# The merge of two mLSTM directions: reciprocal denominators spread by TensorE and applied by VectorE in place of GpSimd

## The chip, the cores and the metric

The kernel runs on one core of a Trainium2 chip. The metric is the device time of one execution in microseconds (us); lower is better. The engines of the core are named as in the profile: PE is TensorE's matmuls and PEld its weight loads, DVE is VectorE, ACT is ScalarE, POOL is GpSimd, SP is SyncE, which here issues the loads of the weights.

## The reference

One layer of a hybrid encoder over 272 positions (16 learned meta tokens and 256 of the sequence), model width 2048, float32. Its output is the 256 sequence positions after a last norm.

```
u = RMSNorm(h); proj = u @ W_in            # q/k, v, o, gates of A; q, k, v of B; two branch gates
branch A: bidirectional mLSTM, 4 heads x 256
branch B: differential attention, 8 heads
merged = sigmoid(g_A) * (A @ W_A) + sigmoid(g_B) * (B @ W_B);  h += merged @ W_out
h += ConvGLU(RMSNorm(h))
```

What matters here is one head of branch A. The reference steps through chunks of 64 positions; over the whole sequence this comes to a matrix of weights for each direction, whose entry for query t and key s is (q_t . k_s) / 16 times a decay. With `den` the sum of a query's weights over the keys,

```
h_fwd[t] = sum_s S_fwd[t, s] v[s] / max(|den_fwd[t]|, exp(-m_fwd[t]))      # s <= t
h_bwd[t] = the same with its own decay, sum, m and keys s >= t
hs = h_fwd + h_bwd;   hn = (hs - mean(hs)) * rsqrt(var(hs) + eps) * norm_g
```

So each direction's weights are divided by a denominator that belongs to the query and the direction, and then both can be added and multiplied by the values in one product.

## The kernel before

**Tiling.** Everything is kept transposed, feature on the partitions and position along the row. Projections are products of a weight block with the layer's input: the weights come as a stream of 512 KB pieces in a fixed order, loaded by SP's queue, split into a high and a low float32r part (`split`: ScalarE casts the high part, L157, VectorE subtracts for the low part, L115), and each 128x128 block takes three matmuls (high x high, high x low, low x high; `product`, L172). One piece of a projection of 256 columns is 24 matmuls. `prepare` splits three pieces ahead of their use, and a raw buffer becomes free for the next load when its low part is done.

**Stages.** `weave` runs two generators step by step, a part of the mLSTM or of the attention in front and a projection behind: each `yield` of the front lets one piece of the projection be traced. The stages in order: queries and keys with the decay terms, values with the heads' weights and their sums (`heads1`), then **`heads2`, the stage of the change, beside the attention's query projection** (`roped(dq, ...)`, 16 pieces in four blocks), then the attention's keys and values, its heads beside the branch gates, the output gate, the merge of the branches, `w_out`, and the FFN. Instructions are issued on each engine in an order that a planner settles when the kernel is built, from the order of the trace and a simulation with its own costs; each engine serves its own list strictly in that order, and semaphores make it wait for others.

**One head's weights.** `FB` is a row of 1034 columns on 128 key partitions that holds six blocks [key, query], three for each direction, one for each key tile (16 meta tokens, two tiles of 128 positions): `PARTS_W` lists column, key tile, first query and width of each: F0 258 wide, F1 256, F2 128, B2 258, B1 130, B0 2 (F0 and B0 on 16 partitions). Queries start at position 14, so there are `NT` = 258. `sums` adds each head's weights over the keys by TensorE into the PSUM tile `den`, head h on partition 32 h, both directions side by side.

**`heads2`.** `rec` = 1 / max(|den|, exp(-m)) is made once for all heads (ScalarE's Abs L665, VectorE's maximum L666 and reciprocal L667). Then for each head:

- `merged`: GpSimd broadcasts partition 32 h of `rec` to all partitions (`rc`, L627) and multiplies each of the six blocks by its stretch of `rc` (six `TENSOR_TENSOR`s on `FB`, which the profile puts at L161, the line of the helper `mul`). VectorE adds the blocks that belong to the same key tile (L164, L634), and the 774 columns that result are split into `hl` (L157 and L115).
- `outputs`: 18 matmuls of values by `hl` into `num`, a tile `two` of PSUM (a pool of two buffers of two banks each). ScalarE squares it (L647) and casts the square's high part (L648), GpSimd subtracts for the low part (L649).
- `normed`: 4 matmuls sum the squares over the partitions (`one`), `rsqrt` follows (ScalarE L151, VectorE L313 to L316), and VectorE multiplies `num` by gain and factor (L660).

The order in the trace is: `merged(0)`, two pieces, and for each head `outputs(h)`, `merged(h + 1)`, two pieces, `normed(h)`, two pieces. `hl` has one buffer.

**Beside it** a block of the query projection ends with `roped`: ScalarE copies out of the accumulator (L692), VectorE shuffles (L696), GpSimd multiplies by the sine table (`u<-u` at L161), VectorE multiplies by the cosine table, adds and splits. So GpSimd's work of the stage is broadcasts and products on `FB`, rope products, and the squares' low parts.

Of the kernel before, what the change touches and what calls it, by code (L numbers as in the profile page):

```python
# [10 lines left out]
F32 = mybir.dt.float32  # L11
# [12 lines left out]
LAM_INIT = 0.2  # L24
# Queries, gates and everything behind them are needed from position 15 on (the last meta token
# reaches position 16 through the FFN's convolution); an even width starts at 14.
T0 = 14
NT = L - T0
FF = 5632
NEG = -1e30  # L30
# Token tiles on partitions: the meta tokens, then the sequence's two halves.
ST = [(0, 16), (16, 128), (144, 128)]
# Columns of the constants' array.
C_ID, C_SEL, C_RC, C_RS, C_E = 0, 128, 640, 912, 1184
C_N = 1186
# Columns of w_in.
Q0, K0, V0, O0, G0 = 0, 1024, 2048, 3072, 4096
DQ0, DK0, DV0, GM0, GD0 = 4112, 5136, 6160, 7184, 9232
# The mLSTM's weights of one head, a [key, query] block per direction (F, B) and key tile, in one row:
# F0 | two columns, F1 | B2 make up the merged weights of the three key tiles; F2, B0, B1 go into them.  # L40
F0c, F1c, B2c, F2c, B0c, B1c, WN = 0, 260, 516, 774, 902, 904, 1034
# [23 lines left out]
def hybrid_layer(ctx, tc, x, meta, norm1_g, w_in, conv_w, gate_bias, mnorm_g, lq1, lk1, lq2, lk2,  # L65
# [26 lines left out]
    def pair(n):  # L92
        """Two 128-row tiles of an operand in two float32r parts."""
        return unit([2, n], F32R), unit([2, n], F32R)
# [22 lines left out]
    @contextmanager  # L117
    def in_order():
        """What is traced inside is issued in its order, engine by engine."""
        traced = nc.cur_bb.bb.instructions  # L120
        start, last = len(traced), {}
        yield
        for i in traced[start:]:
            if i.engine in last:
                behind(i, last[i.engine])
            last[i.engine] = i
# [8 lines left out]
    def activation(out, in_, func, **kw):  # L135
        """Functions of different tables keep the order in which they are traced: few loads of tables."""
        k = KIND[func]
        if k != table[0]:
            before, since[:] = since[:], []
            table[0] = k  # L140
            if k == 0:
                first = S.preload_act_table_set("natural_log_exp_and_others").ins
                for i in before:
                    behind(first, i)
                before = [first]
                since.append(first)
            a = S.activation(out, in_, func, **kw)
            for j in before:
                behind(a.ins, j)
        else:  # L150
            a = S.activation(out, in_, func, **kw)  # L151
            behind(a.ins, since[0])
        since.append(a.ins)
        return a
# [11 lines left out]
    def product(o, terms, first=True, last=True):  # L166
        """o += sum of a.T b, for operands in two parts (an exact one has a single part)."""
        ops = []
        for a, b in terms:
            ops += [(a[0], b[0])] + ([(a[0], b[1])] if len(b) > 1 else []) + ([(a[1], b[0])] if len(a) > 1 else [])  # L170
        for i, (p, q) in enumerate(ops):
            PE.matmul(o, p, q, start=first and i == 0, stop=last and i == len(ops) - 1)  # L172

# [1 line left out]
    blocks = [(w_in, 16, Q0 + 256 * b, 256, 4) for b in range(1, 4)]  # L175
# [57 lines left out]
    def gemm(src, kt, c0, ncols, xs, t0, nt, evac):  # L233
        """Columns c0.. of src, transposed: [column, token]; a generator that stops between pieces."""
        nk = 1024 // ncols
# [23 lines left out]

# [1 line left out]
    table[0] = 0  # L261
# [40 lines left out]
    ones = onesr.bitcast(F32)  # L302
    # a window of 128 columns of it has ones in one column
    selr = const.tile([P, 224], F32R, name="selr")
# [3 lines left out]
    def rsqrt(r, ss, n, work, bias=eps):  # L308
        """1 / sqrt(ss / n + bias), the tables' value and one step of Newton's."""
        a, t = work  # L310
        activation(r, ss, AF.Ln, bias=bias, scale=1.0 / n)
        activation(r, r, AF.Exp, scale=-0.5)
        V.tensor_scalar(out=a, in0=ss, scalar1=1.0 / n, scalar2=bias, op0=ALU.mult, op1=ALU.add)  # L313
        V.scalar_tensor_tensor(out=t, in0=r, scalar=-0.5, in1=r, op0=ALU.mult, op1=ALU.mult)
        mul(t, t, a)
        V.scalar_tensor_tensor(out=r, in0=t, scalar=1.5, in1=r, op0=ALU.add, op1=ALU.mult)  # L316

# [1 line left out]
    n1gT = const.tile([P, 16], F32, name="n1gT")  # L319
# [32 lines left out]
    with in_order():  # L352
# [5 lines left out]
        for k in range(16):  # L358
# [11 lines left out]
            if k == 10:  # L370
                # the gates' 16 columns: both parts side by side
                split(wg[:, :, 0:16], wg[:, :, 16:32], graw)
# [31 lines left out]

# [1 line left out]
    qs, ks = [], []  # L406
# [21 lines left out]

# [1 line left out]
    gsb = r1(L)  # L430
# [6 lines left out]
    def decay_terms():  # L437
        # rows 32 h of [:, direction, :]: head h; the other rows are idle
        pli, plf = two(), two()
# [5 lines left out]
        S.copy(li, pli[:, :, :L])  # L445
        # log_sigmoid(f) = min(f, 0) - log1p(exp(-|f|)), with what 1 + e rounds off given back
        S.activation(e, lf, AF.Abs)
# [13 lines left out]
        yield  # L461
        # m_t = max(lf_t + m_{t-1}, li_t) from 0; the second direction runs backwards
        V.tensor_tensor_scan(out=m[:, 0, :], data0=lf[:, 0, :], data1=li[:, 0, :], initial=0.0, op0=ALU.add, op1=ALU.max)
        V.tensor_tensor_scan(out=m[:, 1, ::-1], data0=lf[:, 1, ::-1], data1=li[:, 1, ::-1], initial=0.0,
                             op0=ALU.add, op1=ALU.max)
        yield
        # rows to broadcast: per key tile, (sum of lf from the tile's edge to t) - m_t
        V.memset(rows[:, 258:260], 0.0)
# [37 lines left out]

# [1 line left out]
    def values(c0, centred):  # L508
# [3 lines left out]
        def put(b):  # L512
# [5 lines left out]
            def turn():  # L518
# [6 lines left out]
                if centred:  # L525
                    # heads' values less their mean over the head: what follows is linear in them
                    mu = sm(3)
# [25 lines left out]

# [1 line left out]
    W, den = [], two()  # L555
# [22 lines left out]
    def scores(h):  # L578
# [3 lines left out]
        for s, (s0, n) in enumerate(ST):  # L582
            # 128 keys for the meta tokens too, whose first 16 rows are used
            product(sc[s], [([t[:, c, s0:s0 + P] for t in ks[h]], [t[:, c, :] for t in qs[h]]) for c in range(2)])
# [35 lines left out]

# [1 line left out]
    hn = []  # L622

    def merged(h, rec):
        FB = W[h]
        rc = t2([2, NT])
        G.partition_broadcast(rc, rec[32 * h:32 * h + 1, :, :])  # L627
        for d, parts in enumerate(PARTS_W):
            for at, s, q, n in parts:
                r = ST[s][1]  # L630
                mul(FB[0:r, at:at + n], FB[0:r, at:at + n], rc[0:r, d, q:q + n], G)
        add(FB[0:16, F0c:F0c + 2], FB[0:16, F0c:F0c + 2], FB[0:16, B0c:B0c + 2])
# [30 lines left out]
    def heads2():  # L663
# [3 lines left out]
        V.reciprocal(rec, rec)  # L667
        hl = merged(0, rec)
        yield
        yield  # L670
        for h in range(4):
            o = outputs(h, hl)
            if h < 3:
                hl = merged(h + 1, rec)
            yield
            yield
            normed(h, *o)
            yield
            yield

# [1 line left out]
    shuffle = [i + 8 if i < 8 else i - 8 if i < 16 else i for i in range(32)]  # L682
# [27 lines left out]

    # lam / max(|lam|, 1) and 1 / max(|lam|, 1): the norm behind takes a scale of its input, eps scaled with it
    lv = t2([4, 64])
# [16 lines left out]
    def softmax(ps, nrow, nmap):  # L729
        """exp(scale (s - max)) and the rows' 1 / sum, for maps [:, m, :] of ps."""  # L730
        p = t2([nmap, L])
# [11 lines left out]
    def position15():  # L743
        """Position 15's queries of all heads and maps at once, on 16 rows; its weights twice, for 14's too."""
        qb = [r1(P, F32R) for _ in range(2)]
# [87 lines left out]

# [1 line left out]
    def gates(dst, c0):  # L835
# [25 lines left out]

# [1 line left out]
    ms = []  # L863
# [20 lines left out]

# [1 line left out]
    hs = []  # L886
# [55 lines left out]

# [1 line left out]
    fc = t2([3, P])  # L944
# [118 lines left out]
```

## Time and profile before

| what | value |
|---|---|
| median of 3 runs | 1638.91 us |
| lowest and highest run | 1638.21, 1639.12 us |
| span of the profiled execution, first to last instruction | 1636.8 us |
| TensorE busy | 1578.3 us, 96% |
| VectorE busy | 1028.0 us, 63% |
| ScalarE busy | 763.5 us, 47% |
| GpSimd busy | 75.7 us, 5% |
| mean granted TensorE clock | 0.981 of full |
| read from HBM | 270.42 MB, 166 GB/s over the span |

The span is the only time that the profile gives for its own execution; the median of the runs is 2.1 us above it, for what lies around the span. Busy time is an average over stages with different limits, and a busy TensorE is not one at its peak, so the stage of the change has to be looked at by itself. In the views, "<- name" behind a wait is what ended it; "issue" means that nothing the profile shows did. PEclk is the clock that TensorE was granted, as a share of full speed (in tenths on the page).

### The profile page before, as it was taken

What the parts mean: (1) busy time and instruction counts of PE and PEld (TensorE: products, weight loads), DVE (VectorE), ACT (ScalarE), POOL (GpSimd) and SP (SyncE); (2) the same over time, 40 slices, a digit from 0 to 9 for tenths busy, and PEclk for the clock granted to TensorE, in tenths of its full rate; (3) what the DMA queues carried; (4) which work ended last, traced back from release to release, by engine and by line L of the source; (5) the groups of instructions that cost most, each with busy time, mean ns of one, the idle gap of its engine ahead of it and who ended that gap; (6) DMA issues with size and microseconds to landing.
All of it is one profiled execution on the core that took longest, in us unless ns stands there. A gap on an engine that the chain in (4) does not pass through costs nothing.

```text
span 1636.8 us, 28921 instructions
## 1 busy us (share of the span) xinstructions
PE 1578.3 (96%) x11862; PEld 1510.2 (92%) x11862; DVE 1028.0 (63%) x1595; ACT 763.5 (47%) x1135; POOL 75.7 (5%) x99
## 2 busy tenths in 40 slices
PE   8999975699999999999999999999999999999998
PEld 7999974699999999999999999999888999999887
DVE  6876644485788655566556766667544566766544
ACT  5656422343455543445555444444433454445433
POOL 0220012110000000000110000000000000000000
PEclk9999986899999999999999999999999999999999
DMA  7464421365445566555555566655555656565562
GB/s 236 135 201 140 132 75 52 92 181 169 129 118 169 181 182 181 181 180 181 189 181 175 180 188 182 185 182 187 184 177 196 189 181 186 179 189 181 178 198 101
DMA packets 254505, 274.39 MB, mean 168 GB/s; under 512 B 11396, under 2 KB 231925, under 8 KB 254357
## 3 DMA queue, kind: packets, MB, share of 16 engines
q1 hardware_dynamic: 248962, 268.99, 53.6%
q10 hardware_dynamic: 5411, 3.56, 0.8%
q8 instruction: 93, 1.52, 0.4%
q14 instruction: 39, 0.32, 0.1%
HBM read 270.42 MB, written 2.10 MB: 166 GB/s over the span
## 4 chain that ended last, share of the span: by engine, by line
PE 82%; issue 14%; POOL 2%; DVE 0%; DMA 0%; ACT 0%; POOLq 0%; SPq 0%; DVEq 0%
PE acc L172 78%; PE two L172 1%; POOL FB L161 1%; PE two L778 1%; POOL FB L564 0%; PE two L900 0%; PE one L790 0%; POOL u L161 0%; DMA xc<-in_x_dram 0%; PE two L333 0%; POOL t L627 0%; POOL t L649 0%; POOL FB L561 0%; PE two L911 0%; PE one L172 0%
## 5 line engine op out<-in xcount | busy, mean ns | idle before, releaser
L172 PE MATMUL acc<-u,hi 128*128 128x258 f32 (+1 forms) x6656 | 1226.8, 286 | 1.3 <-ACT u L692 1.3
L172 PEld LDWEIGHTS acc<-u,hi 128*128 128x128 f32 x6656 | 1037.6, 191 | 5.5 <-ACT u L692 1.9
L172 PE MATMUL acc<-u,lo 128*128 128x258 f32 (+1 forms) x3328 | 938.3, 285 | 1.9 <-DVE lo L115 1.9
L115 DVE TENSOR_TENSOR lo<-raw,hi 128x1024 fp32r<-128x1024 f32 x499 | 615.3, 1235 | 439.9 <-ACT hi L157 437.9
L157 ACT CAST hi<-raw 128x1024 fp32r<-128x1024 f32 x499 | 523.0, 1049 | 649.6 <-PE acc L172 502.2
L172 PEld LDWEIGHTS acc<-u,lo 128*128 128x128 f32 x3328 | 628.1, 190 | 3.7 <-DVE lo L115 3.0
L172 PE MATMUL acc<-hi,u 128*128 128x512 f32 (+1 forms) x704 | 210.6, 382 | 0.0
L172 PEld LDWEIGHTS acc<-hi,u 128*128 128x128 f32 x704 | 129.8, 188 | 27.7
L172 PE MATMUL acc<-lo,u 128*128 128x512 f32 (+1 forms) x352 | 134.5, 382 | 0.0
L172 PEld LDWEIGHTS acc<-lo,u 128*128 128x128 f32 x352 | 66.2, 188 | 14.6
L172 PE MATMUL two<-hl,v 16*128 16x258 f32 x24 | 8.2, 429 | 41.0 <-ACT hl L157 41.0
L161 DVE TENSOR_TENSOR r<-acc,r 128x258 f32<-128x258 f32 x88 | 37.3, 423 | 13.6 <-PE acc L172 13.6
L172 PEld LDWEIGHTS two<-hl,v 16*128 16x128 f32 x24 | 5.0, 253 | 43.4 <-ACT hl L157 41.8
L157 ACT CAST u<-r 128x256 fp32r<-128x256 f32 (+2 forms) x93 | 34.7, 405 | 12.6 <-DVE r L161 7.0
L115 DVE TENSOR_TENSOR u<-r,u 128x256 fp32r<-128x256 f32 (+2 forms) x93 | 37.7, 436 | 3.9 <-ACT u L157 3.3
L959 ACT ACTIVATE r<-r,fcT 128x256 f32<-128x256 f32 x88 | 39.8, 500 | 0.0
L960 DVE SCALAR_TENSOR_TENSOR r<-r,fcT,r 128x256 f32<-128x256 f32 x88 | 38.5, 479 | 0.0
L961 DVE SCALAR_TENSOR_TENSOR r<-r,fcT,r 128x255 f32<-128x255 f32 x88 | 38.5, 479 | 0.0
L157 ACT CAST hl<-FB 128x1034 fp32r<-128x1034 f32 (+1 forms) x8 | 7.6, 945 | 54.4 <-DVE FB L164 48.0
L151 ACT ACTIVATE r<-r 128x256 f32<-128x256 f32 (+2 forms) x77 | 29.6, 413 | 5.7 <-DVE r L419 5.3
L164 DVE TENSOR_TENSOR FB<-FB 128x128 f32<-128x128 f32 (+1 forms) x12 | 4.8, 412 | 41.6 <-POOL FB L161 41.6
L164 POOL TENSOR_TENSOR ssum<-ssum,r 128x258 f32<-128x258 f32 x15 | 13.4, 896 | 318.5 <-ACT r L927 318.0
(232 smaller groups left out, 767.7 us busy)
## 6 DMA issues: line engine op xcount, KB each, us to landing
raw<-in_w_in_dram SPq DMA_DIRECT2D x176, 512.0 KB, 3.7
raw<-in_w_up_dram SPq DMA_DIRECT2D x176, 512.0 KB, 3.6
raw<-in_w_down_dram SPq DMA_DIRECT2D x88, 512.0 KB, 3.7
raw<-in_w_out_dram SPq DMA_DIRECT2D x32, 512.0 KB, 3.5
raw<-in_w_branch_m_dram SPq DMA_DIRECT2D x16, 512.0 KB, 3.5
raw<-in_w_branch_d_dram SPq DMA_DIRECT2D x16, 512.0 KB, 3.4
xc<-in_x_dram SPq DMA_DIRECT2D x4, 512.0 KB
t<-in_x_dram ACTq DMA_DIRECT2D x8, 256.0 KB
```

The lines of the kernel that those rows point to most:

```text
L115: V.tensor_tensor(out=out, in0=src, in1=hi.bitcast(F32), op=ALU.subtract)
L151: a = S.activation(out, in_, func, **kw)
L157: S.copy(hi, src)
L161: eng.tensor_tensor(out=o, in0=a, in1=b, op=ALU.mult)
L164: eng.tensor_tensor(out=o, in0=a, in1=b, op=ALU.add)
L172: PE.matmul(o, p, q, start=first and i == 0, stop=last and i == len(ops) - 1)
L778: PE.matmul(ps[:, i, 0:L], dq[h // 2][p][o:o + 64, h % 2, 2 + P * qt:2 + P * (qt + 1)], dk[h // 2][q][o:o + 64, h % 2, :], start=(p, q) == ...
L959: S.activation(z, u[:, 2:NT], AF.Copy, scale=fcT[:, 1, f:f + 1])
L960: V.scalar_tensor_tensor(out=z, in0=u[:, 1:NT - 1], scalar=fcT[:, 0, f:f + 1], in1=z, op0=ALU.mult, op1=ALU.add)
L961: V.scalar_tensor_tensor(out=z[:, 0:SEQ - 1], in0=u[:, 3:NT], scalar=fcT[:, 2, f:f + 1], in1=z[:, 0:SEQ - 1], op0=ALU.mult, op1=ALU.add)
```

## The change

`rec` is split into two float32r parts, `rhl`. A new constant tile `rowr` holds, for each head, a 128x128 block of zeros with ones in row 32 h; GpSimd sets it with five `memset`s. `spread(h, rhl)` multiplies that block with both parts of both directions (four matmuls for a head), which puts head h's reciprocals on all partitions of a PSUM tile `rc`, from the pool `two`. `merged` no longer uses GpSimd: VectorE multiplies the blocks by `rc` straight from PSUM, F0 and F1 in one instruction of 2 x 258 columns (F1 is laid out so that its column of query q is 258 further on), then B1, B0, F2 and B2, all on 128 partitions. The additions, the split, `outputs` and `normed` are as before. The order in the trace becomes: split of `rec`, one piece, `spread(0)` and `merged(0)`, two pieces, and for each head `spread(h + 1)`, `outputs(h)`, one piece, `merged(h + 1)`, `normed(h)`, three pieces. Comments and docstrings go out of the file; what the instructions of other stages do is unchanged.

```diff
-    def merged(h, rec):
+    rowr = unit([4, P], F32R)
+    G.memset(rowr.bitcast(F32), 0.0)
+    for h in range(4):
+        G.memset(rowr[32 * h:32 * h + 1, h, :].bitcast(F32), 1.0)
+
+    def spread(h, rec):
+        rc = two()
+        for d in range(2):
+            product(rc[:, d, 0:NT], [((rowr[:, h, :],), [t[:, d, :] for t in rec])])
+        return rc
+
+    def merged(h, rc):
         FB = W[h]
-        rc = t2([2, NT])
-        G.partition_broadcast(rc, rec[32 * h:32 * h + 1, :, :])
-        for d, parts in enumerate(PARTS_W):
-            for at, s, q, n in parts:
-                r = ST[s][1]
-                mul(FB[0:r, at:at + n], FB[0:r, at:at + n], rc[0:r, d, q:q + n], G)
+        F01 = FB[:, F0c:F0c + 516].rearrange("p (s q) -> p s q", s=2)
+        mul(F01, F01, rc[:, 0:1, 0:NT].to_broadcast([P, 2, NT]))
+        for at, d, q, n in ((B1c, 1, 0, 130), (B0c, 1, 0, 2), (F2c, 0, 130, 128), (B2c, 1, 0, 258)):
+            mul(FB[:, at:at + n], FB[:, at:at + n], rc[:, d, q:q + n])
...
         V.reciprocal(rec, rec)
-        hl = merged(0, rec)
+        rhl = pair(NT)
+        split(*rhl, rec)
+        yield
+        hl = merged(0, spread(0, rhl))
         yield
         yield
         for h in range(4):
+            if h < 3:
+                rc = spread(h + 1, rhl)
             o = outputs(h, hl)
+            yield
             if h < 3:
-                hl = merged(h + 1, rec)
-            yield
-            yield
+                hl = merged(h + 1, rc)
             normed(h, *o)
             yield
             yield
+            yield
```

## Rows read from the trace of the kernel before

**Rows 1.** The page's 40 slices: TensorE's busy tenths and its granted clock.

```profile
PE   8999975699999999999999999999999999999998
PEclk9999986899999999999999999999999999999999
```

**Rows 2.** Windows of core 0, us from the span's start, with their columns.

```profile
core 0: us, PE busy (x) PEld busy (x) DVE busy (x) ACT busy (x) POOL busy (x), PEclk, DMA share, GB/s
200.00:325.40 125.40, 83.12 (x530) 77.86 (x530) 53.69 (x81) 35.52 (x52) 27.17 (x36) 0.77 0.26 73
222.30:241.30 19.00, 17.71 (x92) 16.19 (x92) 6.06 (x10) 4.09 (x8) 2.13 (x2) 0.68 0.20 56
330.00:360.00 30.00, 30.00 (x242) 30.00 (x241) 24.71 (x32) 15.56 (x20) 5.17 (x3) 1.00 0.62 178
```

**Rows 3.** Waits of 200 to 330 us: total us, times, longest.

```profile
PE two L172 <- ACT hl L157: 41.0, 4, 12.7
ACT hl L157 <- DVE FB L164: 48.0, 4, 14.8
DVE FB L164 <- POOL FB L161: 41.6, 4, 12.6
POOL FB L161 <- issue: 29.3, 4, 7.6
POOL t L627 <- issue: 18.4, 3, 6.3
```

**Rows 4.** GpSimd's timeline: start, duration, operation, in brackets idle before and its releaser.

```profile
207.64 1.67 POOL L627 PARTITION_BROADCAST t<-u  x1 [116.87 <-DVE u L667]
216.88 2.87 POOL L161 TENSOR_TENSOR FB<-FB,t 16x258 f32<-16x258 f32 x6 [7.58 <-issue]
240.19 0.85 POOL L627 PARTITION_BROADCAST t<-u  x1 [6.28 <-issue]
321.40 1.30 POOL L649 TENSOR_TENSOR t<-t,t 128x516 fp32r<-128x516 f32 x1 [6.29 <-ACT t L648]
```

**Rows 5.** TensorE's timeline: start, duration, operation.

```profile
203.25 0.40 PE L172 MATMUL acc<-u,hi 128*128 128x258 f32 x2
217.65 0.40 PE L172 MATMUL acc<-u,hi 128*128 128x258 f32 x2
```

**Rows 6.** Groups of instructions by shape, 190 to 330 us: busy us, mean ns.

```profile
L161 DVE TENSOR_TENSOR u<-u 128x516 f32<-128x516 f32 x4 | 2.8, 695 | 0.1
L588 DVE SCALAR_TENSOR_TENSOR FB<-two,FB 128x258 f32<-128x258 f32 x1 | 0.4, 419 | 0.0
L588 DVE SCALAR_TENSOR_TENSOR FB<-two,FB 128x130 f32<-128x130 f32 x1 | 0.3, 284 | 0.0
L634 DVE COPY FB<-FB 128x2 f32<-128x2 f32 x4 | 0.6, 155 | 0.0
L115 DVE TENSOR_TENSOR u<-u 128x516 fp32r<-128x516 f32 x4 | 2.7, 684 | 0.0
L648 ACT CAST t<-t 128x516 fp32r<-128x516 f32 x4 | 2.5, 623 | 0.1
L161 POOL TENSOR_TENSOR u<-u 128x516 f32<-128x516 f32 x4 | 6.2, 1553 | 8.9 <-DVE u L696 7.9 <-DVE FB L164 1.0
L649 POOL TENSOR_TENSOR t<-t,t 128x516 fp32r<-128x516 f32 x4 | 5.2, 1298 | 31.2 <-ACT t L648 31.2
```

**Rows 7.** Timelines of VectorE and GpSimd around two subtractions on hl.

```profile
252.13 1.64 POOL L161 TENSOR_TENSOR u<-u 128x516 f32<-128x516 f32 x1 [1.01 <-DVE FB L164]
252.92 1.67 DVE L115 TENSOR_TENSOR hl<-FB,hl 128x774 fp32r<-128x774 f32 x1 [0.20 <-ACT hl L157]
281.03 0.95 DVE L115 TENSOR_TENSOR hl<-FB,hl 128x774 fp32r<-128x774 f32 x1
```

**Rows 8.** Timelines of TensorE and VectorE: last head's outputs and norm.

```profile
319.03 1.00 PE L172 MATMUL two<-hl,u 128*128 128x258 f32 x6
329.38 0.88 DVE L660 SCALAR_TENSOR_TENSOR u<-two,prmT,r 128x258 f32<-128x258 f32 x2
```

More of the change, by code (lines that the diff above doesn't have):

```diff
@@ L671, in heads2 @@
         for h in range(4):
+            if h < 3:
+                rc = spread(h + 1, rhl)
             o = outputs(h, hl)
+            yield
             if h < 3:
-                hl = merged(h + 1, rec)
+                hl = merged(h + 1, rc)
+            normed(h, *o)
             yield
-            yield
-            normed(h, *o)
             yield
```

## The prediction, made before the changed kernel ran

> **What bounds the kernel now.** I read the page from the top. TensorE is busy almost throughout and runs at full clock except between about 200 and 330 us [rows 1]; so a change is worth what it does to TensorE in that stretch, and I look nowhere else for a gain. The windows then say how large the hole is [rows 2]: in the 125.4 us from 200 to 325.4, TensorE has work in 83.1 us only, at a mean granted clock of 0.77, while VectorE is busy 53.7 us and GpSimd 27.2 us. So 125.4 - 83.1 = 42.3 us are stops. At full clock three matmuls of a piece start every 0.36 us: from 203.25 to 217.65 there are 40 such threes in 14.40 us, 0.120 us for a matmul [rows 5]. The 530 matmuls of the stretch would therefore need 63.6 us; they were busy 83.1, so the low clock costs 19.5 us more. It falls behind each stop, to the lower of its two levels (1.2 in place of 2.4 GHz): the stretch behind the first stop, 222.3 to 241.3, has a mean of 0.68 [rows 2]. Stops and clock together: 42.3 + 19.5 = 61.8 us.
>
> The chain of waits names the stops [rows 3]: TensorE waits four times, 41.0 us, for ScalarE's cast to `hl`; that one waits for VectorE's additions to `FB`, these for GpSimd's products on `FB`. GpSimd itself waits 29.3 and 18.4 us before its products and its broadcasts, and what ends these waits is "issue", nothing that another engine did. The GpSimd timeline shows where [rows 4]: the first broadcast (207.64) starts when the reciprocals are there, the products that follow it (216.88) start 7.6 us after its end; a broadcast that follows a `TENSOR_TENSOR` (240.19) comes after 6.3 us. Between two `TENSOR_TENSOR`s there is no such gap: the one at 321.40 starts when ScalarE's cast releases it. So each change between broadcast and arithmetic costs GpSimd some 6 to 7.6 us of nothing, twice for each head (once for the first), and TensorE stands behind it. The real work in the chain is small: a broadcast 0.85 to 1.67 us, six products 2.87 us.
>
> **The change part by part.** *Removed:* four broadcasts and 24 products on GpSimd. With them go the changes between the two kinds, since all that GpSimd does in the stretch is then `TENSOR_TENSOR` (the rope products and the squares' low parts, 4 each, 6.2 + 5.2 = 11.4 us [rows 6]). The seven gaps come to 29.3 + 18.4 = 47.7 us, more than the 41.0 us that TensorE waited [rows 3]. So without the gaps the order as it stood would have kept TensorE supplied; that is the main reason to believe that the stops go entirely and not by a part.
>
> *Added on TensorE:* for each head two products of two matmuls (high and low part), 128x258: 16 at 0.120 = 1.9 us, on the path, since TensorE sets the pace.
>
> *Added on VectorE:* per head one product of 516 elements (0.695, as VectorE's 128x516 product) and four of 130, 2, 128 and 258 (0.284, 0.155, 0.284, 0.419), together 1.84 us; four heads 7.35 us. Three of these prices come from products that already read PSUM, so I add nothing for the source [rows 6]. Once, the low part of the reciprocals, 0.68 us, and on ScalarE their high part, 0.62 us. VectorE in the stretch: 53.7 + 7.35 + 0.68 = 61.7 us. TensorE would need 63.6 + 1.9 = 65.5. VectorE is nowhere near the path today; afterwards it has 94% of TensorE's time. It serves in order: the five products wait for TensorE's spread, and behind them stand the low parts of the weights, for which TensorE and the loads of raw weights wait in turn.
>
> *Contention.* VectorE's subtraction on `hl` took 0.95 us at 281.03, but 1.67 us at 252.92, where GpSimd's product of 252.13 ran until 253.77 [rows 7]: of 0.85 us of overlap it lost 0.72. If every one of GpSimd's remaining 11.4 us held VectorE up, VectorE would need 61.7 + 11.4 = 73.1 us, 7.6 more than TensorE; if none did, TensorE stays the bound. Against full price speaks the stretch 330 to 360: VectorE 24.7 and GpSimd 5.2 of 30 us, and TensorE never stops [rows 2]. I take 6 us, nearer to the full price because the one pair of rows that shows it is near it; the ends are 0 and 7.6. The Trainium skill ("SBUF — State Buffer", section "Who interferes with whom") says that a VectorE instruction with two inputs in SBUF and a GpSimd instruction that reads SBUF shut each other out, and that one with a single SBUF input does not contend. By that rule the sum would take the full 7.6 us, from the subtractions alone, since the new products have one of their inputs in PSUM; the pair of rows agrees with its first half, and no row here shows the second.
>
> *Moved and at nothing:* the five `memset`s that make the selecting rows stand on GpSimd ahead of its first product, where it idles 116.9 us until 207.6 [rows 4]; without that cover they would cost at most five passes of 1.55 us [rows 6]. The first head's chain becomes: cast 0.62, subtraction 0.68, spread 0.5, products 1.84, additions about 0.9, cast 0.84: 5.4 us, where today the products alone begin 9.2 us after the broadcast does (207.64 to 216.88). One more piece of the projection is set ahead of it. `rc` moves from SBUF to the PSUM pool of two buffers that also holds the heads' outputs `num`: the output product of head h + 1 now has to wait until head h is normed. That chain (square, cast, GpSimd's low part, sum, Ln, Exp, six on VectorE) took from 320.03, the end of the last output product, to 330.26, 10.2 us [rows 8]. Four pieces of 24 matmuls, 11.5 us, and 8 matmuls of sums and spreads, 1.0 us, lie between; it is covered with 2.3 us to spare. No DMA is added, and none is issued by VectorE or GpSimd here.
>
> *Sum.* 61.8 gone, 1.9 added, 6 left over: 53.9 us less. The profiled span is 1636.8 us, so 1582.9; the median of the runs is 1638.9, 2.1 more for what lies around the span, so 1585.0 us.
>
> **The rivals.** *Stops gone, TensorE at full clock (the forecast).* From 1579 (nothing left over) to 1590 (twice the contention I take). 69 in 100.
>
> *VectorE becomes the bound.* Its 73.1 us, and for each head some 2 us in which its queue stands at the products until TensorE's spread comes through (four, 8 us): 81 us in place of 125.4. That gives 1594, and 1590 to 1600 around it. For it: 94% of TensorE's time and work in order. Against it: 330 to 360. 17 in 100.
>
> *The two PSUM buffers.* The 2.3 us to spare are lost if the norm's VectorE work queues 5 us behind splits; then three stops of some 3 us, each with the low clock behind it (19.5 us for four stops, so 5 each): 24 us, 1603 to 1615. Against it: the 10.2 us were taken with weights' splits already queued in between, and the wait is over in that time. 10 in 100.
>
> *The change doesn't do what it says:* GpSimd's gaps also come between its remaining instructions. Eight of 7.2 us, with VectorE's rope sum waiting behind four of them, eat up the gain: 1637. Against it: the instruction at 321.40 [rows 4]. 2 in 100.
>
> *Slower.* One mechanism: each head's chain lies bare, none of the four pieces between. Spread to `hl` with its low part (0.5 + 1.84 + 0.9 + 0.84 + 0.95 = 5.0) and the norm (10.2) make 15.2 us for a head, 61 us for four, and 19.5 for the clock, 80 against the 61.8 removed: with the 1.9 added 1659. It decides from 10.1 us bare for a head, (59.9 - 19.5) / 4. Against it: the four pieces hang on neither chain, only on weights and their own accumulators. 2 in 100.
>
> **How the numbers follow.** The time is that of the first case, 1585, its own range 1579 to 1590. With VectorE as the bound 86 in 100 are held; I end at 1602, where the third case begins, and start at 1578, a microsecond under the case with nothing left over. This kernel's runs tell 0.2%, 3.3 us, from no change. All of the first three cases are faster, 96 in 100; I give 95 to faster, 3 to the same (the fourth, and mixtures near it), 2 to slower.
>
> **What would show it.** Right: no GpSimd broadcast behind 90 us and no GpSimd wait ended by "issue" between 200 and 330; TensorE's clock at 1.00 in every stretch; sixteen new matmuls on `two`; VectorE's 516-wide product near 0.70 us and VectorE above 85% busy for some 65 to 75 us; the rest of the kernel as before, 55 us earlier. Wrong: TensorE stopped on `hl` or on `num` for over 3 us at a head with the clock down behind it (buffers), many short stops on weights' low parts (VectorE), or GpSimd gaps that remain.

## The result, and the profile after

The changed kernel takes 1593.56 us (median of 4 runs, 1592.96 to 1594.1) against 1639.01 us before: a ratio of 0.973, 95% interval 0.9717 to 0.9743, 45.5 us less. The span of its profiled execution is 1592.3 us, 44.5 less than before. That lies inside the predicted range (1578 to 1602) and above the predicted time (1585) and the likeliest case's own range (1579 to 1590).

The page of the changed kernel, its 40 slices of 39.8 us each, answers to [rows 1]:

```profile
PE   8999989999999999999999999999999999999997
PEclk9999989999999999999999999999999999999999
```

Three dark slices have become one, the sixth. GpSimd's timeline answers to [rows 4] (start, duration, operation, in brackets the idle time before and its releaser):

```profile
90.70 0.52 POOL L626 MEMSET u<- 128x512 f32 x1
91.27 0.95 POOL L628 MEMSET u<- 1x128 f32 x4
...
210.17 1.20 POOL L161 TENSOR_TENSOR u<-u 128x516 f32<-128x516 f32 x1 [117.94 <-DVE u L713]
229.34 1.54 POOL L661 TENSOR_TENSOR t<-t,t 128x516 fp32r<-128x516 f32 x1 [17.97 <-ACT t L660]
...
264.04 1.30 POOL L661 TENSOR_TENSOR t<-t,t 128x516 fp32r<-128x516 f32 x1 [7.46 <-issue]
```

No broadcast is left in the stage; the `memset`s are made at 90.7, under cover. The one wait that still says "issue" is no gap of the old sort: the cast that this subtraction needs (ScalarE, 263.29, 0.62 us) ended at 263.91, 0.13 us before it starts.

VectorE's new products, in the groups by shape of 200 to 285 us (count, then busy us and mean ns), answer to [rows 6]:

```profile
L161 DVE TENSOR_TENSOR FB<-FB,two 128x516 f32<-128x516 f32 x4 | 2.7, 679 | 0.3 <-PE two L172 0.3
L161 DVE TENSOR_TENSOR FB<-FB,two 128x258 f32<-128x258 f32 x4 | 1.6, 409 | 0.0
L161 DVE TENSOR_TENSOR FB<-FB,two 128x130 f32<-128x130 f32 x4 | 1.1, 276 | 0.0
L161 DVE TENSOR_TENSOR FB<-FB,two 128x128 f32<-128x128 f32 x4 | 1.1, 274 | 0.0
L161 DVE TENSOR_TENSOR FB<-FB,two 128x2 f32<-128x2 f32 x4 | 0.6, 142 | 0.0
L172 PE MATMUL two<-u 128*128 128x258 f32 x16 | 2.8, 288 | 0.0
```

0.68 + 0.41 + 0.28 + 0.27 + 0.14 = 1.78 us a head against the 1.84 of the prediction, and 16 matmuls of spread as counted. Now the windows of the stage (their columns as in [rows 2]):

```profile
200.00:280.00 80.00, 75.76 (x545) 71.66 (x544) 63.59 (x119) 37.20 (x58) 11.86 (x8) 0.91 0.39 118
230.00:243.50 13.50, 10.97 (x46) 9.82 (x46) 7.69 (x14) 5.01 (x10) 3.36 (x3) 0.51 0.00 0
243.50:280.00 36.50, 36.50 (x286) 35.38 (x285) 31.95 (x60) 19.80 (x30) 6.64 (x4) 0.99 0.52 157
```

TensorE stands still for 80 - 75.76 = 4.2 us of the stage, against 42.3 us before [rows 2], and runs at the lower clock from 230 to 243.5 only. VectorE is busy 63.6 of 80 us. The place is in the timelines, TensorE first:

```profile
224.30 0.28 PE L172 MATMUL acc<-u,lo 128*128 128x258 f32 x1
...
226.40 0.98 PE L172 MATMUL two<-hl,u 128*128 128x258 f32 x6
228.79 0.38 PE L172 MATMUL two<-hl,v 16*128 16x258 f32 x1 [1.42 <-ACT hl L157]
...
232.65 1.66 PE L172 MATMUL two<-hl,u 128*128 128x258 f32 x6
...
237.21 0.55 PE L172 MATMUL one<-t,ones 128*128 128x258 f32 x1 [2.26 <-ACT u L709]
...
238.84 0.63 PE L172 MATMUL acc<-u,hi 128*128 128x258 f32 x2
```

ScalarE, and one line of VectorE:

```profile
227.91 0.83 ACT L157 CAST hl<-FB 128x774 fp32r<-128x774 f32 x1
...
234.84 0.83 ACT L157 CAST hl<-FB 128x774 fp32r<-128x774 f32 x1
...
236.77 0.65 ACT L709 COPY u<-acc 128x258 f32<-128x258 f32 x2
...
236.59 0.48 DVE L313 TENSOR_SCALAR r<-one,eps 128x258 f32<-128x258 f32 x1
```

The last projection matmul of the stretch is at 224.30, the next at 238.84. Between them stand the outputs of head 0 (to 227.4) and, next to them in TensorE's list, those of head 1 (228.79 to 234.3). `hl` has one buffer, so the cast for head 1 (227.91) begins when head 0's outputs are done, and that for head 2 (234.84) when head 1's are; in ScalarE's list the square of those outputs stands just ahead of each. From 230 the clock is at the lower level, and two groups of six matmuls show the price: 0.98 us at full clock, 1.66 us there.

### The profile page after: what moved, and what is told of

It is laid out like the page before. It is cut to its first block, busy times and chain, and to the rows that moved or that the text cites. A ratio compares the mean times of both kernels' runs of the same rounds, so it can differ in the third digit from the quotient of the medians.

```text
span 1592.3 us, 28944 instructions
## 1 busy us (share of the span) xinstructions
PE 1571.7 (99%) x11878; PEld 1505.2 (95%) x11878; DVE 1034.1 (65%) x1616; ACT 763.8 (48%) x1136; POOL 62.1 (4%) x76
## 4 chain that ended last, share of the span: by engine, by line
PE 97%; DVE 1%; ACT 1%; DMA 0%; issue 0%; POOL 0%; SPq 0%; DVEq 0%; POOLq 0%; ACTq 0%
PE acc L172 90%; PE two L172 3%; PE two L795 1%; PE one L172 0%; DVE lo L115 0%; PE two L917 0%; PE one L807 0%; PE two L523 0%; DMA xc<-in_x_dram 0%; PE two L333 0%; PE two L928 0%; ACT hi L157 0%; PE one L333 0%; PE two L915 0%; ACT hl L157 0%
## 5 line engine op out<-in xcount | busy, mean ns | idle before, releaser
L161 DVE TENSOR_TENSOR r<-r,r 128x256 f32<-128x256 f32 (+1 forms) x57 | 22.1, 421 | 0.1
L161 DVE TENSOR_TENSOR r<-acc,u 128x258 f32<-128x258 f32 x32 | 13.5, 422 | 12.8 <-PE acc L172 12.8
L161 POOL TENSOR_TENSOR u<-u 128x516 f32<-128x516 f32 (+1 forms) x8 | 14.0, 1752 | 176.1 <-DVE u L713 165.9
L161 DVE TENSOR_TENSOR r<-acc,rB 128x272 f32<-128x272 f32 (+1 forms) x40 | 17.0, 430 | 5.4 <-PE acc L172 5.4
```

The costliest lines, as they stand in the source:

```text
L161: eng.tensor_tensor(out=o, in0=a, in1=b, op=ALU.mult)
```

## The experiments

All times are medians; each ratio is to the kernel before, run beside it on the same chip (1636.5 to 1639.0 us).

| run | us | ratio, 95% interval | what it changes |
|---|---|---|---|
| changed kernel | 1593.56 | 0.973 (0.9717 to 0.9743) | |
| `bcast_first` | 1606.99 | 0.9818 (0.9804 to 0.9833) | before, four broadcasts first |
| `spread_pool` | 1591.65 | 0.9725 (0.971 to 0.9739) | changed, products on GpSimd |
| `bcast_dve` | 1606.36 | 0.9812 (0.9795 to 0.9828) | changed, spread by GpSimd's broadcast |
| `hl_two` | 1590.24 | 0.9717 (0.9703 to 0.9732) | changed, second place for `hl` |
| `late_spread` | 1589.81 | 0.9701 (0.9685 to 0.9718) | changed, spread behind the outputs |
| `copy_dve` | 1592.95 | 0.9723 (0.9709 to 0.9738) | changed, copies on VectorE |
| `no_pool` | 1592.10 | 0.9716 (0.9702 to 0.9731) | changed, no GpSimd beside it |
| `order_before` | 1587.38 | 0.9686 (0.9671 to 0.97) | changed, trace order of before |
| `ob_pool` | 1589.56 | 0.9703 (0.9688 to 0.9717) | `order_before`, products on GpSimd |
| `ob_hl2` | 1585.30 | 0.9682 (0.9668 to 0.9697) | `order_before`, second place for `hl` |
| `order_only` | 1619.09 | 0.9883 (0.9867 to 0.99) | before, the change's order |
| `no_extra` | 1597.91 | 0.976 (0.9747 to 0.9774) | changed, without the extra piece |

### What was in the way: GpSimd's changes of kind, or its work?

**`bcast_first`:** the kernel before, its broadcasts together.

```diff
         V.reciprocal(rec, rec)
+        row, rec = rec, [unit([2, NT]) for _ in range(4)]
+        for h in range(4):
+            G.partition_broadcast(rec[h], row[32 * h:32 * h + 1, :, :])
```

> The kernel before with one thing changed: GpSimd makes its four broadcasts one after another ahead of the first head, into four tiles, and the products stay on GpSimd. Theory 1 (the stops were GpSimd's changes between broadcast and arithmetic): one change is left, some 7.5 us ahead of the first head, and the three later stops (36.9 us and most of the low clock behind them) go: 1590 to 1600 us. Theory 2 (the stops were GpSimd's slow work itself, the 24 products of 2.87 us a head and the broadcasts): all of that work is still there, so the time stays within some 10 us of before, 1628 to 1639.

It took 1606.99 us, 30.5 less than before: theory 2's 1628 or more is ruled out, theory 1's 1590 to 1600 was too hopeful. GpSimd's timeline has one gap where seven stood (5.3 us of waiting ahead of a low part at 271.87 also say "issue", but end 0.13 us behind the cast that it needs):

```profile
207.50 4.02 POOL L669 PARTITION_BROADCAST u<-u  x4 [116.68 <-DVE u L666]
218.26 6.78 POOL L161 TENSOR_TENSOR FB<-FB,u 16x258 f32<-16x258 f32 x12 [6.74 <-issue]
...
226.15 10.38 POOL L161 TENSOR_TENSOR FB<-FB,u 16x258 f32<-16x258 f32 x12
```

What I had not reckoned with is the length of the two lines of products: all four heads' are made one after another, 6.78 + 10.38 = 17.2 us with one rope product between, and TensorE has little to do in that time (2.1 us busy of 220 to 230).

**`spread_pool`:** the changed kernel with the 24 products back on GpSimd.

```diff
     def merged(h, rc):
         FB = W[h]
-        F01 = FB[:, F0c:F0c + 516].rearrange("p (s q) -> p s q", s=2)
-        mul(F01, F01, rc[:, 0:1, 0:NT].to_broadcast([P, 2, NT]))
-        for at, d, q, n in ((B1c, 1, 0, 130), (B0c, 1, 0, 2), (F2c, 0, 130, 128), (B2c, 1, 0, 258)):
-            mul(FB[:, at:at + n], FB[:, at:at + n], rc[:, d, q:q + n])
+        rs = t2([2, NT])
+        S.copy(rs, rc[:, :, 0:NT])
+        for d, parts in enumerate(PARTS_W):
+            for at, s, q, n in parts:
+                r = ST[s][1]
+                mul(FB[0:r, at:at + n], FB[0:r, at:at + n], rs[0:r, d, q:q + n], G)
```

> The changed kernel, but the spread reciprocals are copied from PSUM to SBUF by ScalarE and the products stay on GpSimd as six a head. Theory 1 (changes between broadcast and arithmetic): no broadcast is left in the stage, so no change of kind either, and the time is that of the changed kernel with some 3 us a head of longer chain, mostly covered: 1590 to 1600. Theory 2 (GpSimd's slow work): the products are the larger part of that work and remain, so most of the 45 us comes back: 1620 or more.

1591.65 us: as fast as the changed kernel. GpSimd goes from a low part to products and back without a gap (three waits that say "issue", 3.8 to 4.5 us, each end within 0.14 us of the cast that the low part needs):

```profile
228.46 1.29 POOL L663 TENSOR_TENSOR t<-t,t 128x516 fp32r<-128x516 f32 x1 [9.26 <-ACT t L662]
229.70 3.23 POOL L161 TENSOR_TENSOR FB<-FB,t 16x258 f32<-16x258 f32 x6
```

So the half of the change that moves the products to VectorE brings nothing that can be told; the spread by TensorE, which takes the broadcasts away, brings the gain. It doesn't need the change's order: `ob_pool`, below, keeps the order of before and GpSimd's products, and takes 48.3 us less than before. Theory 1 is shown, theory 2 has fallen.

**`bcast_dve`:** the other half alone, products on VectorE, spread by GpSimd.

```diff
     def spread(h, rec):
-        rc = two()
-        for d in range(2):
-            product(rc[:, d, 0:NT], [((rowr[:, h, :],), [t[:, d, :] for t in rec])])
+        rc = t2([2, NT])
+        G.partition_broadcast(rc, rec[32 * h:32 * h + 1, :, :])
         return rc
```

> The changed kernel, but the reciprocals are spread by GpSimd's broadcast into SBUF instead of by TensorE; the products are VectorE's. Theory 1: GpSimd still alternates between broadcasts and the rope products and low parts, each change some 6 to 7.5 us; a broadcast has a whole head's time ahead of its use, so a part is covered: 1600 to 1625. Theory 2 (slow products): they are off GpSimd, so the time is that of the changed kernel, 1590 to 1597.

1606.36 us, theory 1's range, outside theory 2's. The gaps are there, around each broadcast:

```profile
234.87 0.85 POOL L628 PARTITION_BROADCAST t<-u  x1 [5.74 <-issue]
242.62 1.26 POOL L655 TENSOR_TENSOR t<-t,t 128x516 fp32r<-128x516 f32 x1 [6.90 <-issue]
249.59 0.85 POOL L628 PARTITION_BROADCAST t<-u  x1 [5.71 <-issue]
258.31 1.18 POOL L161 TENSOR_TENSOR u<-u 128x516 f32<-128x516 f32 x1 [7.87 <-issue]
```

Now it is the norm's low part that waits, and TensorE behind it (5.2 us, on `one`). VectorE's products wait for two of the broadcasts (7.8 and 9.4 us), and TensorE stands another 5.7 us for L313, which comes behind the first of these products in VectorE's list.

**`order_only`:** the kernel before with the order of the change.

```diff
+    def spread(h, rec):
+        rc = t2([2, NT])
+        G.partition_broadcast(rc, rec[32 * h:32 * h + 1, :, :])
+        return rc
...
-        hl = merged(0, rec)
+        yield
+        hl = merged(0, spread(0, rec))
         yield
         yield
         for h in range(4):
+            if h < 3:
+                rc = spread(h + 1, rec)
             o = outputs(h, hl)
+            yield
             if h < 3:
-                hl = merged(h + 1, rec)
-            yield
-            yield
+                hl = merged(h + 1, rc)
             normed(h, *o)
             yield
             yield
+            yield
```

> The kernel before with the change's order alone: broadcast and products stay on GpSimd, one piece ahead of the first head, the broadcast of head h + 1 ahead of outputs(h), its products one piece behind. If GpSimd's changes of kind stay as many (broadcast and arithmetic still alternate): some of them move out of the chain, since the broadcast is no longer last in it: 1610 to 1630. If the order has no part in the gain: 1634 to 1640.

1619.09 us, 18.8 less. The first two broadcasts now stand together, so two of the seven gaps go; the five others measure 5.9 to 7.1 us, and TensorE still stops 25.9 us (before: 42.3). The time lies in the first of the two ranges; the order is no neutral part of the change. GpSimd's timeline:

```profile
207.73 2.34 POOL L626 PARTITION_BROADCAST t<-u  x2 [116.88 <-DVE u L670]
217.15 8.27 POOL L161 TENSOR_TENSOR FB<-FB,t 16x258 f32<-16x258 f32 x12 [7.07 <-issue]
...
241.54 0.84 POOL L626 PARTITION_BROADCAST t<-u  x1 [5.87 <-issue]
249.26 2.86 POOL L161 TENSOR_TENSOR FB<-FB,t 16x258 f32<-16x258 f32 x6 [6.88 <-issue]
```

### What is left of the stop

**`no_pool`:** the prediction's contention, taken away.

```diff
-        G.tensor_tensor(out=lo, in0=sq, in1=hi.bitcast(F32), op=ALU.subtract)
+        low(lo, sq, hi)
...
-                    mul(sw, sw, table(1), G)
+                    mul(sw, sw, table(1), V if dst is dq else G)
```

> The changed kernel, with the query projection's rope products and the squares' low parts on VectorE too, so GpSimd does no arithmetic in the stage until the keys. VectorE gets 4 x 0.7 + 4 x 0.7 = 5.6 us more work and loses the contention of 11.4 us of GpSimd. The prediction's term (contention leaves some 6 us): 2 to 6 us less, 1588 to 1592. VectorE's load as the bound: 4 to 6 us more, 1597 to 1600. Theory C (order): whatever the new order of the outputs makes of it, within 3 us of the changed kernel if the bunch stays.

1592.10 us, 1.5 less, and the intervals overlap. Of GpSimd's 11.9 us in the stage 1.3 are left and VectorE has 65.6 us to do there, yet TensorE stops nearly as long:

```profile
200.00:280.00 80.00, 76.48 (x562) 72.36 (x561) 65.63 (x131) 38.19 (x59) 1.26 (x1) 0.94 0.44 123
```

The range for VectorE's load as the bound (1597 to 1600) is ruled out; the one for contention (1588 to 1592) ends 0.1 us short of the time. The edit takes contention away and adds load, so the time alone could hide one behind the other. The trace shows little of either: TensorE's stops are 3.5 us in place of 4.2, and the longest is again 2.3 us, for the same L313 behind the subtraction for head 2's `hl`. So contention is a small part at most of what is left, 1.5 us by this run.

**`hl_two`:** a second place for `hl`.

```diff
-        hl = rbs.tile([P, 2, WN], F32R, tag="w", name="hl")
-        hi, lo = hl[:, 0, :], hl[:, 1, :]
+        if h % 2 == 0:
+            hl = rbs.tile([P, 2, WN], F32R, tag="w", name="hl")
+            hi, lo = hl[:, 0, :], hl[:, 1, :]
+        else:
+            hi, lo = (rbp.tile([P, WN], F32R, tag="rb", name="hl") for _ in range(2))
```

> The changed kernel with a second place for hl: odd heads split into two tiles of the pool of FB, whose buffers are free by then. Theory A (what is left of the stop, from 226.5 to 244 us, comes from the single buffer of hl: ScalarE's cast for the next head waits for TensorE's outputs, and the accumulators' copies stand behind it): the stop and the low clock behind it go, 8 to 14 us less: 1580 to 1586. Theory B (VectorE's load and its contention with GpSimd set what is left, as the prediction had it): no change beyond 3 us: 1590 to 1597. Theory C (two heads' outputs stand next to each other in TensorE's order, whatever the buffers): a smaller gain, 1586 to 1592, with the outputs of heads 0, 1 and 2 still without pieces of the projection between them.

1590.24 us, 3.3 less, with intervals that overlap. TensorE no longer waits for `hl`; but the outputs of heads 0 and 1 are now adjacent without a pause (224.16 to 230), and three shorter stops and the low clock follow (231 to 240). Theory A has fallen. The time lies in the ranges of B and of C, but C's sign is there, the outputs side by side; `no_pool` speaks against B.

**`copy_dve`:** the projection's copies out of the accumulators on VectorE.

```diff
-                S.copy(u[:, ci, :], a)
+                (V.tensor_copy if dst is dq else S.copy)(u[:, ci, :], a)
```

> The changed kernel, with the copies of the query projection out of the accumulators on VectorE instead of ScalarE, eight of some 0.4 us. Theory C' (of the two parts of theory C, the copies' place in ScalarE's queue is what holds TensorE): the copies come earlier, TensorE goes on with the projection: 1582 to 1588. If the outputs' bunching itself is what counts, the copies now stand in VectorE's queue behind the split of hl, which waits as long: 1590 to 1596. Theory B (VectorE's load): 3 us more load, 1594 to 1598.

1592.95 us: nothing. And it corrects a reading: the wait of 2.3 us ahead of `one` is there again, now put down to VectorE:

```profile
PE one L172 <- DVE r L313: 2.3, 1, 2.3
```

In the changed kernel L313, which reads head 0's sum out of the single bank `one`, ended at 237.07, 0.14 us before TensorE's matmul at 237.21; the copy that the profile names there merely ended at about the same time. L313 stood in VectorE's list behind the subtraction for head 2's `hl`, this behind the cast of 234.84. Theory C' has fallen; the time is in the range that was given for the bunching. (In this run TensorE also waits once, 1.1 us, for a head's `num` to be normed.)

**`late_spread`:** spread of head h + 1 held behind outputs(h) on TensorE (`mm` lists the matmuls of `product` as they are traced, `behind` fixes an order without a wait).

```diff
-            if h < 3:
-                rc = spread(h + 1, rhl)
             o = outputs(h, hl)
+            end = len(mm)
+            if h < 3:
+                rc = spread(h + 1, rhl)
+                behind(mm[end], mm[end - 1])
```

> The changed kernel, with TensorE's spread of head h + 1 held in its order behind the last matmul of outputs(h), so that the merges can't run ahead of the outputs. Theory C (what is left of the stop comes from two heads' outputs standing next to each other, while the copies out of the accumulators wait in ScalarE's queue behind these heads' casts and squares): pieces of the projection come between the outputs, the stop from 226.5 to 244 us goes: 1580 to 1586. Theory B (VectorE's load and contention, the prediction's term): no change beyond 3 us, or slower.

1589.81 us, 3.7 less, with intervals that just overlap, and above theory C's range. The outputs of heads 0 and 1 (from 223.27 and from 230.19) still stand next to each other, with no projection matmul from 223.3 to 235.9, so the edit did not do what it was for.

**`order_before`:** the change's engines in the trace order of before.

```diff
         split(*rhl, rec)
-        yield
...
-            if h < 3:
-                rc = spread(h + 1, rhl)
             o = outputs(h, hl)
-            yield
             if h < 3:
-                hl = merged(h + 1, rc)
+                hl = merged(h + 1, spread(h + 1, rhl))
+            yield
+            yield
             normed(h, *o)
             yield
             yield
-            yield
```

> The changed kernel with the trace order of before: no piece ahead of the first spread, spread(h + 1) and merged(h + 1) right behind outputs(h), two pieces, normed(h), two pieces. If the order of the trace that came with the change matters for what is left: 5 us or more to either side of 1593.6. If the planner decides by what is ready: within 3 us, the outputs of two heads still side by side.

1587.38 us, 6.2 less than the changed kernel, and the intervals are apart. The outputs of heads 0 and 1 stand some 11 us from each other, with projection between them, the clock stays up, and one stop of 2.7 us is left, on a copy out of an accumulator. The stage's window:

```profile
200.00:280.00 80.00, 77.27 (x594) 73.44 (x593) 63.81 (x125) 37.83 (x59) 13.32 (x9) 1.00 0.44 127
```

TensorE's timeline there:

```profile
214.42 0.51 PE L172 MATMUL acc<-u,hi 128*128 128x258 f32 x2 [2.73 <-ACT u L706]
...
218.36 0.50 PE L172 MATMUL two<-hl,v 16*128 16x258 f32 x2
218.78 0.99 PE L172 MATMUL two<-hl,u 128*128 128x258 f32 x6
219.70 0.62 PE L172 MATMUL two<-hl,v 16*128 16x258 f32 x3
220.25 0.98 PE L172 MATMUL two<-hl,u 128*128 128x258 f32 x6
221.07 0.64 PE L172 MATMUL two<-u 128*128 128x258 f32 x4
...
229.42 0.99 PE L172 MATMUL two<-hl,u 128*128 128x258 f32 x6
```

TensorE does 594 matmuls in the 80 us, 49 more than in the changed kernel; at 0.120 us [rows 5] that is 5.9 us. VectorE has the same 63.8 us and GpSimd the same kind of work, so these were not the bound.

**`no_extra`:** the changed kernel without its extra piece.

```diff
         split(*rhl, rec)
-        yield
         hl = merged(0, spread(0, rhl))
```

> The changed kernel with one line less: the yield behind the split of the reciprocals, so that no extra piece of the projection goes ahead of the first spread; the rest of the change's order stays (spread of head h + 1 ahead of outputs(h), one piece, merged and normed, three pieces). If the extra piece is what puts the end of a block of the projection right ahead of the first outputs (so that its accumulators' copies queue behind two heads' casts): 1585 to 1589, like order_before. If the place of the spreads and merges is what bunches the outputs: 1591 to 1596, like the changed kernel.

1597.91 us, 4.4 more than the changed kernel, the intervals apart, and outside both ranges: the extra piece is not what costs, it helps. Without it TensorE waits 3.7 us, in two stops on `two`, for VectorE's products; and the outputs of heads 0 and 1 stand side by side all the same, from 216.2 to 231.2, with TensorE at the lower clock throughout 220 to 230.

**`ob_pool`** is `order_before` with the edit of `spread_pool`, **`ob_hl2`** with that of `hl_two`.

> The changed kernel in the trace order of before (as order_before) and with the products back on GpSimd, six a head, from an SBUF copy that ScalarE makes of the spread reciprocals. If where the products run doesn't matter (only GpSimd's changes between broadcast and arithmetic did): within 3 us of order_before, 1584 to 1591. If VectorE's products from PSUM bring something of their own once the order is right (the chain is some 2.9 - 1.5 + 0.6 = 2 us a head longer with GpSimd): 1592 to 1600.

> The changed kernel in the trace order of before, with a second place for hl. One stop of 2.7 us is left in order_before, at a copy out of an accumulator, and no stop on hl: so the buffer should bring nothing, 1585 to 1590. If the single hl buffer still costs something in the order of before: 1580 to 1584.

1589.56 and 1585.30 us, each in the range for a part that doesn't matter. Both intervals overlap with that of `order_before`: with the better order, too, it can't be told where the products run, nor that `hl` wants a second place. `ob_hl2` has the lowest median of all.

## Why the prediction was right, and where it was not

**The cause** was right: the stops were GpSimd's changes between broadcast and arithmetic. `spread_pool` and `ob_pool` show it most plainly, since all of GpSimd's products stay and the gain does too, in either order. The Trainium skill ("GPSIMD Engine Reference", section "2.1 Instruction dispatch") says that the first call of a freshly loaded routine pays some 6 us for loading its code, with no instruction in the profile; the gaps here are 5.7 to 6.3 us ahead of a broadcast and 6.7 to 7.9 us ahead of arithmetic, at each change. That code is loaded in them, and at each change, is a guess from that page, which speaks of the first call; the runs show the gaps and what makes them go, not what fills them.

**"The stops go entirely"** was the step that failed. It argued from the gaps' sum, 47.7 us against 41.0 us of waits, that the order as it stood would keep TensorE supplied. For that order it was nearly so: `order_before` keeps one stop of 2.7 us. But the change also altered the order, and the planner then put two heads' outputs side by side. I took "four pieces lie between" from the order of the trace; TensorE's list had none between the outputs of heads 0 and 1.

**The 6 us left over** were a mis-sized term with the wrong cause. Against the working's span with nothing left over, 1636.8 - 59.9 = 1576.9, the changed kernel's 1592.3 is 15.4 us more: 4.2 of stops; 46 matmuls in 10.97 us between 230 and 243.5, 5.4 more than at 0.120; and, as `order_before` shows at full clock, 17 matmuls of an outputs product in 2.71 us (218.36 to 221.07), 0.159 each, so that four heads' 72 need 2.8 us more than I priced (0.6 of it counted in the 5.4 already). That was to be seen in [rows 8], where six take 1.00 us. Another 0.5 us comes from the keys' matmuls, 116 of the 530 and 272 columns wide, which take 0.124 us each ([rows 2]: 242 in 30.00 us). So what I put down to the low clock, 19.5 us, was in part work that is there at any clock. The last 3 us I can't place.

The contention that I had put in their stead is real, but next to nothing on TensorE's path: `no_pool` takes it away, for some 5.6 us more of VectorE's work by estimate, and the time moves by 1.5 us, within the intervals. By the rule of the Trainium skill that I weighed ("SBUF — State Buffer", section "Who interferes with whom"), the sum would have taken the full 7.6 us. The trace of the changed kernel agrees with the rule as far as contention shows: VectorE's addition, 0.69 us elsewhere, takes 1.78 us beside a subtraction of GpSimd. But TensorE didn't wait for it:

```profile
255.28 1.30 POOL L661 TENSOR_TENSOR t<-t,t 128x516 fp32r<-128x516 f32 x1
255.36 1.78 DVE L164 TENSOR_TENSOR u<-u 128x516 f32<-128x516 f32 x1 [1.10 <-POOL u L161]
```

That the measured time lies inside the stated range is in part luck: it is above the end of the likeliest case, 1590, and inside only because the range ran on to 1602 for VectorE as the bound, which did not come.

**The rivals.** VectorE as the bound (1590 to 1600) has the measured time in its range and not its mechanism: VectorE is busy 63.6 of 80 us, and in `order_before` the same load goes with a TensorE that never waits for it. VectorE does hold TensorE once in the changed kernel, the 2.3 us on L313, but by the order of its list: it had idled 6.0 us for ScalarE's cast just before. The two PSUM buffers showed no wait in the changed kernel; in `copy_dve` (1.1 us) and `no_extra` (3.7 us) TensorE did wait on `two` for VectorE, so they are near the path. That the gaps remain, and slower, fell with the result. Of the signs I listed, the clock at 1.00 in every stretch and VectorE above 85% did not come true.

**The clock's price**, 5 us for a stop, was about right: without the outputs' and the keys' own time, the low clock behind a cluster of stops cost some 4.8 us here (5.4 - 0.6), and some 16 us for four stops before (19.5 - 2.8 - 0.5).

**Still open:** which of the two parts of `order_before` (merges in the step of the outputs, or two and two pieces) keeps the outputs apart; `no_extra` only says that the third, the extra piece, does not.

## What to carry to other kernels

An engine that waits for nothing the profile names, always ahead of the same kind of instruction, pays for changing between kinds: count the changes, and put together or take away the rarer kind, before moving the work itself, which was free here. When a change takes a stall out of a stage whose order a planner settles, read the new order in the trace: the order that came with the change cost 6 us of the gain, where taking the contention away moved the time by 1.5. And price each product by its own rows, not by the stage's commonest.

## What the runs showed of the hardware that was not expected

- GpSimd pays at a change between broadcast and `TENSOR_TENSOR` in both directions (5.7 to 6.3 and 6.7 to 7.9 us), but not from broadcast to `AFFINE_SELECT`, as the changed kernel's timeline shows, where the one ends at 78.47 and the other has begun at 78.30:

```profile
72.40 6.07 POOL L561 PARTITION_BROADCAST FB<-rows  x4 [33.35 <-issue]
78.30 12.44 POOL L564 TENSOR_SCALAR_AFFINE_SELECT FB<-FB 16x2 f32<-16x2 f32 x24
```

- At least part of a change runs while the instruction's own wait goes on. In `bcast_dve` the rope product at 258.31 starts 7.87 us after the broadcast's end (250.44), although the shuffle whose output it reads ended only at 252.65 (the line below); a whole change behind that, 6.7 us or more, would have ended at 259.3 or later. Whether it costs something to go from `memset` to `TENSOR_TENSOR` no run shows: 118 us lie between them in the changed kernel.

```profile
251.91 0.74 DVE L706 STREAM_SHUFFLE u<-u 128x516 f32<-128x516 f32 x1
```

- Matmuls of the outputs product, which read `hl` in a different 258-column stretch with 16 or 128 rows in turn, take 0.159 us each at full clock, those of the projection 0.120. By the starts in `order_before`, those with 16 rows take the longer, 0.18 to 0.21 us, those with 128 rows 0.14 to 0.15; whether the number of rows or the stretch does it, no run shows.
